# Pacing the modulation columns over a whole feed-forward half, the latent part of its last slab included

## The chip, the cores and the metric

One core of a Trainium2 chip runs the program. The metric is the device time of one execution in microseconds, as the median of several runs. One more execution was profiled; its time and its span, from the first instruction to the last, are given beside the runs.

## What is computed

Two layers of a diffusion backbone run over 256 context tokens and 256 latent tokens of width 1024, in float32. Each layer is a half-step SwiGLU feed-forward, a token mixer (gated DeltaNet, differential attention and SSD on one input, merged by gates), and a second half-step feed-forward. Each of the three is modulated by columns that come from a conditioning vector: nine groups of 1024 per layer and per kind of token.

```python
for i in range(DEPTH):                       # 2
    mx = (silu(c) @ w_ada[i] + b_ada[i]).reshape(bsz, 9, 1, 1024)     # latent tokens
    mc = (silu(c_ctx) @ w_ada[i] + b_ada[i]).reshape(9, 1024)         # context tokens
    x = x + half_ffn(x, ng[0], ng[1], mx[:, 0], mx[:, 1], mx[:, 2], w_ffn_in[i, 0], w_ffn_out[i, 0])
    ctx = ctx + half_ffn(ctx, ng[0], ng[1], mc[0], mc[1], mc[2], w_ffn_in[i, 0], w_ffn_out[i, 0])
    hx = modulate(rms_norm(x, ng[2]), mx[:, 3], mx[:, 4])             # h * (1 + scale) + shift
    hc = modulate(rms_norm(ctx, ng[2]), mc[3], mc[4])
    yx, yc = token_mixing(hx, hc, not last, ...)
    x = x + mx[:, 5] * rms_norm(yx, ng[3])
    x = x + half_ffn(x, ng[4], ng[5], mx[:, 6], mx[:, 7], mx[:, 8], w_ffn_in[i, 1], w_ffn_out[i, 1])
    ...                                      # the same for ctx, except in the last layer
# half_ffn(h, ...) = 0.5 * gate * rms_norm(swiglu(modulate(rms_norm(h, g_pre), shift, scale), w1, w2), g_post)
```

The result is x after both layers.

## The kernel before

Below, ffn(l, 0) and ffn(l, 1) are the two feed-forward halves of layer l, and mix(l) is the mixer between them. A segment is the 256 context tokens (segment 0) or the 256 latent ones (segment 1).

**Products.** Every weight block goes the same way (`wload`, from L133). A DMA on SyncE's queue brings it into a `raw` tile (three of them), ScalarE rounds it into a hi tile `whi` (L93), and VectorE writes the remainder into a lo tile `wlo` (L102); there are two of each. TensorE multiplies with both (L114): for each of eight contraction steps the hi weight by the hi and the lo activations, then the lo weight by the hi activations. In the mixer every third weight block uses a pair of `araw` tiles for hi and lo in the place of `whi` and `wlo`.

**A feed-forward half** (`ffn`). The 22 tiles of 128 hidden columns are cut into three slabs of 8, 7 and 7. For each hidden tile the inner function `hidden` makes two products from two weight blocks. ScalarE applies Silu to the first (`gS`), VectorE multiplies the two (`gV`, L96), ScalarE rounds `gV` into a `B` tile (L93), and VectorE writes the lo part of it into another (L102). When a slab's hidden tiles are done, eight output products follow that read all of the slab's `B` tiles. Slabs 0 and 1 take both segments together. Slab 2 takes them one after the other: first the context, whose end (`tail(0)`: norm of the output, addition to x, norm for the next stage) is then woven piece by piece into the latent part through `rest`, and then the latent tokens, whose end is woven into the next stage. The first `early` hidden tiles of slab 0 are made by segment too.

**Norms** (`rms`, from L370). TensorE sums the squares over the partitions, GpSimd raises to the power (L382), and VectorE writes a diagonal (L111) into a `gx` tile, which TensorE multiplies with ones to spread it over the partitions.

**Modulation columns** (`ada_block`, from L272). The list `todo` holds blocks in the order of their use, (layer, group, one of eight contraction steps). A block is one DMA of 512 KB into an `araw` tile, of which there are two, and then four scalar_tensor_tensor instructions on VectorE (L291): for each kind of token and each half of the block one product with the condition and a sum along the row, which goes into the columns `mod` or `part`. The elementwise product itself is not used. For the latent tokens it is written back over the `araw` tile, for the context tokens into a `gx` tile, of which there are two, the same two that the diagonals take in turn. Where only the latent tokens need the columns, a block has two instructions. After the eighth block of a group four small additions bring in `part` and the bias. `ada_block` also starts the next block's DMA.

**What sets the pace.** `due` is the number of blocks up to the half's goal: 48 in ffn(0,0), 40 in ffn(0,1), 40 in ffn(1,0), and none in ffn(1,1). Each `tick(share)` adds share times `due` to a credit and issues a block for each whole unit of it. A block is issued with a shifted priority, so that the scheduler may place it ahead of work that was written earlier, as far as its tiles are free. `whole` is the number of shares: two for a hidden tile of slabs 0 and 1 beyond the `early` ones, one for an output product of these slabs, and in slab 2 one for a hidden tile and a half for an output product, but in the context part only. `need(l, j)` issues at once whatever blocks up to (l, j) are still missing.

The vectors, masks and tables that mix(0) reads are loaded behind the DMA of the last modulation block (`vectors`, L227).

Of the kernel before, what the change touches and what calls it, by code (L numbers as in the profile page):

```python
# [58 lines left out]
class Net:  # L59
# [388 lines left out]
    def ffn(self, l, half, hl, segs, tail, mid):  # L448

        io = self.io
        y = [None] * KD
        one = [(s * SEG, (s + 1) * SEG) for s in segs]
        both = (one[0][0], one[-1][1])
        goal = ((0, 7), (1, 3), (1, 8), (1, 8))[2 * l + half]
        self.due, self.credit = sum(e[:2] <= goal for e in self.todo), 0
        self.left = self.due  # L460
        if self.due and (l, half) != (0, 0):
            self.ada_load(segs)
        early = 4 + 2 * l + half if len(segs) == 2 else 0
        whole = 2 * (15 - early) + 16 + (11 if len(segs) == 2 else 0)

        def hidden(k, k0, gu, a, b):
            pg, pu = self.proj([io["w_ffn_in"][l, half, k, i] for i in range(2)], hl, a, b)
            sg = self.t("gS", [P, T], 2)
            self.act(sg[:, a:b], pg[:, a:b], AF.Silu)
            f = self.t("gV", [P, T], 2)  # L470
            self.mul(f[:, a:b], sg[:, a:b], pu[:, a:b])
            hi, lo = self.rows(gu, k - k0, a, b)
            self.split(hi, lo, f[:, a:b])

        for si, (k0, k1) in enumerate(SLABS):
            nk = k1 - k0
            gu = self.newh()
            if si == 0:
                self.pace = 4
                for a, b in one:  # L480
                    for k in range(early):
                        with self.tc.issue_after(self.first.ins) if self.first else nullcontext():
                            hidden(k, k0, gu, a, b)
                        self.first = None
                    self.rest(None)
                    self.pace = 0
            src = io["w_ffn_out0"][l, half] if si == 0 else io["w_ffn_out1"][l, half, si - 1]
            for a, b in one if si == 2 else [both]:
                for k in range(k0 + (early if si == 0 else 0), k1):
                    hidden(k, k0, gu, a, b)  # L490
                    self.rest(2)
                    if si < 2:
                        self.tick(2 / whole)
                    elif a == 0:
                        self.tick(1 / whole)
                acc = {}
                for m in range(KD):
                    w = self.wload(src[m], nk * P)
                    o = self.ps("mm")
                    self.gemm(o[:, a:b], w, nk, P, gu, a, b, late=m == 0)  # L500
                    if si == 0:
                        y[m] = self.p()
                        self.act(y[m][:, a:b], o[:, a:b])
                    else:
                        self.add(y[m][:, a:b], y[m][:, a:b], o[:, a:b])
                    self.rest(1)
                    if si == 2:
                        self.squares(y, a // SEG, m, acc)
                        if a == 0:
                            self.tick(0.5 / whole)  # L510
                    else:
                        self.tick(1 / whole)
                if si == 2:
                    self.later(tail(a // SEG, y, acc))
            if si == 1:
                mid()


    def small_proj(self, l, hl):
# [987 lines left out]
```

## Time and profile before

| | us |
|---|---|
| three runs | 2545.96, 2547.03, 2553.83 |
| median | 2547.03 |
| the profiled execution | 2554.7 |
| its span | 2552.9 |
| TensorE busy in the span | 2431.2 |
| VectorE busy | 1820.8 |
| ScalarE busy | 1161.4 |
| GpSimd busy | 289.8 |

The profiled execution is one of its own, 7.7 us above the median of the others. Busy times leave out register, branch and DMA-issuing instructions. TensorE's weight loads run beside its products and are counted apart. In the rows further down PE is TensorE, DVE is VectorE, ACT is ScalarE and POOL is GpSimd; what stands in brackets at a row's end is the idle time of the engine before it and what ended that. Neighbouring rows overlap a little, since an engine starts an instruction before the one ahead of it has ended.

### The profile page before, as it was taken

The page shows a single profiled execution, that of the slowest core. Times are in us where ns is not written, and L with a number is a line of the kernel's source. Part 1 is how long each engine was busy: PE and PEld are TensorE (multiplying, and loading weights), DVE is VectorE, ACT ScalarE, POOL GpSimd, SP SyncE. Part 2 cuts the span into 40 slices and gives each one's busy share as a digit, 9 for nine tenths or more (in the row PEclk, how much of TensorE's full clock was granted, in tenths as well). Part 3 has the DMA queues.
Part 4 walks back from the last instruction along what each step waited for, and adds up shares of the span by engine and source line. Part 5 has one row for each costly group of instructions (what it writes and reads, how often), then busy time and mean ns, then how long its engine had stood idle before and what let it go on. Part 6 is the DMA issues. An engine that isn't in the chain of part 4 may idle for free. (4 is left out here: it accounts for less than half of the span.)

```text
span 2552.9 us, 40594 instructions
## 1 busy us (share of the span) xinstructions
PE 2431.2 (95%) x15546; PEld 2125.0 (83%) x15546; DVE 1820.8 (71%) x3826; ACT 1161.4 (45%) x1935; POOL 289.8 (11%) x288
## 2 busy tenths in 40 slices
PE   5999999999999999989999999999999889998998
PEld 3978799777788767888889998889988779887997
DVE  6888558899874564588964798634788977665455
ACT  4422256656443443563323563223566544454443
POOL 2000002202100011220000230000231120011001
PEclk8999999999999999999999999999999999998999
DMA  7766456443212312656754558734554342443664
GB/s 249 229 212 219 152 178 202 141 149 96 88 58 67 132 59 81 186 162 224 246 159 152 181 179 270 258 99 150 179 185 139 92 110 92 157 132 119 189 187 134
DMA packets 150498, 401.62 MB, mean 157 GB/s; under 512 B 39584, under 2 KB 50592, under 8 KB 150304
## 3 DMA queue, kind: packets, MB, share of 16 engines
q1 hardware_dynamic: 150304, 399.03, 49.8%
q8 instruction: 122, 2.00, 0.3%
q14 instruction: 72, 0.59, 0.1%
HBM read 383.76 MB, written 15.20 MB: 156 GB/s over the span
## 5 line engine op out<-in xcount | busy, mean ns | idle before, releaser
L114 PE MATMUL mm<-B,whi 128*128 128x256 f32 (+1 forms) x7632 | 1337.7, 325 | 28.8 <-ACT B L93 11.6
L114 PEld LDWEIGHTS mm<-B,whi 128*128 128x128 f32 x7632 | 1123.1, 190 | 155.7 <-ACT B L93 15.4
L93 ACT ACTIVATE whi<-raw 128x1024 fp32r<-128x1024 f32 (+1 forms) x506 | 524.5, 1037 | 611.9 <-PE mm L114 558.0
L102 DVE TENSOR_TENSOR wlo<-raw,whi 128x1024 fp32r<-128x1024 f32 (+1 forms) x506 | 613.4, 1213 | 177.1 <-ACT whi L93 147.1
L114 PE MATMUL mm<-B,wlo 128*128 128x256 f32 (+1 forms) x3816 | 696.6, 322 | 5.9 <-DVE wlo L102 5.9
L114 PEld LDWEIGHTS mm<-B,wlo 128*128 128x128 f32 x3816 | 567.3, 189 | 65.2 <-DVE wlo L102 7.7
L114 PE MATMUL mm<-B,araw 128*128 128x512 f32 (+1 forms) x1104 | 225.3, 352 | 4.2 <-DVE araw L102 4.2
L114 PEld LDWEIGHTS mm<-B,araw 128*128 128x128 f32 x1104 | 177.3, 191 | 31.4 <-DVE araw L102 5.6
L291 DVE SCALAR_TENSOR_TENSOR araw<-araw,P 128x512 f32<-128x512 f32 x264 | 173.0, 686 | 26.8 <-DMA araw<-in_w_ada 26.8
L291 DVE SCALAR_TENSOR_TENSOR gx<-araw,P 128x512 f32<-128x512 f32 x200 | 131.3, 687 | 44.5 <-DMA araw<-in_w_ada 44.0
L99 POOL TENSOR_TENSOR gm<-gm,ge 128x256 f32<-128x256 f32 x33 | 33.7, 1020 | 1127.0 <-ACT ge L93 1127.0
L93 ACT ACTIVATE B<-gV 128x256 fp32r<-128x256 f32 (+1 forms) x124 | 58.1, 469 | 226.2 <-DVE gV L96 226.1
L96 DVE TENSOR_TENSOR gV<-gS,mm 128x256 f32<-128x256 f32 (+1 forms) x124 | 59.7, 482 | 114.2 <-PE mm L114 99.7
L99 DVE TENSOR_TENSOR P<-P,mm 128x256 f32<-128x256 f32 (+1 forms) x88 | 43.2, 491 | 105.5 <-PE mm L114 105.5
L105 DVE SCALAR_TENSOR_TENSOR cv<-xp,vec,cv 128x512 f32<-128x512 f32 (+1 forms) x160 | 111.6, 706 | 2.1 <-ACT cv L93 1.4
L93 ACT ACTIVATE gS<-mm 128x256 f32<-128x256 f32 (+1 forms) x172 | 75.5, 439 | 35.8 <-PE mm L114 33.8
L102 DVE TENSOR_TENSOR araw<-raw,araw 128x1024 fp32r<-128x1024 f32 x56 | 70.0, 1251 | 25.8 <-PE mm L114 13.7
L93 ACT ACTIVATE araw<-raw 128x1024 fp32r<-128x1024 f32 x56 | 59.3, 1059 | 59.5 <-PE mm L114 43.2
L99 POOL TENSOR_TENSOR P<-P,gV 128x512 f32<-128x512 f32 (+1 forms) x30 | 36.1, 1202 | 241.6 <-DVE gV L105 238.1
L102 DVE TENSOR_TENSOR B<-gV,B 128x256 fp32r<-128x256 f32 (+1 forms) x124 | 62.3, 503 | 0.0
L93 ACT ACTIVATE B<-gR,mod 128x256 fp32r<-128x256 f32 x88 | 42.8, 501 | 33.5 <-DVE gR L105 33.1
L102 POOL TENSOR_TENSOR B<-gK,B 128x256 fp32r<-128x256 f32 x44 | 44.1, 1002 | 87.6 <-ACT gK L93 87.6
(265 smaller groups left out, 2180.7 us busy)
## 6 DMA issues: line engine op xcount, KB each, us to landing
raw<-in_w_ffn_in SPq DMA_DIRECT2D x248, 512.0 KB, 3.8
raw<-in_w_in SPq DMA_DIRECT2D x144, 512.0 KB, 3.6
araw<-in_w_ada SPq DMA_DIRECT2D x132, 512.0 KB, 4.4
raw<-in_w_ffn_out SPq DMA_DIRECT2D x88, 448.0 KB, 3.3
raw<-in_w_ffn_out SPq DMA_DIRECT2D x32, 512.0 KB, 4.3
raw<-in_w_branch SPq DMA_DIRECT2D x24, 512.0 KB, 3.5
raw<-in_w_out SPq DMA_DIRECT2D x24, 512.0 KB, 3.9
P<-keep SPq DMA_DIRECT2D x20, 256.0 KB, 5.5
```

The lines of the kernel that those rows point to most:

```text
L93: self.nc.scalar.activation(out=out, in_=in_, func=func, **kw)
L96: (eng or self.nc.vector).tensor_tensor(out, a, b, op=ALU.mult)
L99: (eng or self.nc.vector).tensor_tensor(out, a, b, op=ALU.add)
L102: (eng or self.nc.vector).tensor_tensor(out, a, b, op=ALU.subtract)
L105: self.nc.vector.scalar_tensor_tensor(out, a, s, b, op0=op0, op1=op1)
L114: self.nc.tensor.matmul(out, lhsT=lhsT, rhs=rhs, start=start, stop=stop)
L291: self.nc.vector.scalar_tensor_tensor(o, wh, 1.0, self.cond[s][h], op0=ALU.mult, op1=ALU.mult, accum_out=c)
```

## The change

`whole` now has 11 shares for each segment in the half, so both parts of slab 2 count: 60 shares instead of 49 in ffn(0,0), 58 instead of 47 in ffn(0,1), and 56 instead of 45 in ffn(1,0). The latent part of slab 2 ticks as the context part does. At the end of the half `need` issues what would be left up to the goal. No block is added or taken out.

```diff
--- before.py
+++ after.py
@@ -461,7 +461,7 @@
         if self.due and (l, half) != (0, 0):
             self.ada_load(segs)
         early = 4 + 2 * l + half if len(segs) == 2 else 0
-        whole = 2 * (15 - early) + 16 + (11 if len(segs) == 2 else 0)
+        whole = 2 * (15 - early) + 16 + 11 * len(segs)
 
         def hidden(k, k0, gu, a, b):
             pg, pu = self.proj([io["w_ffn_in"][l, half, k, i] for i in range(2)], hl, a, b)
@@ -491,7 +491,7 @@
                     self.rest(2)
                     if si < 2:
                         self.tick(2 / whole)
-                    elif a == 0:
+                    else:
                         self.tick(1 / whole)
                 acc = {}
                 for m in range(KD):
@@ -506,14 +506,14 @@
                     self.rest(1)
                     if si == 2:
                         self.squares(y, a // SEG, m, acc)
-                        if a == 0:
-                            self.tick(0.5 / whole)
+                        self.tick(0.5 / whole)
                     else:
                         self.tick(1 / whole)
                 if si == 2:
                     self.later(tail(a // SEG, y, acc))
             if si == 1:
                 mid()
+        self.need(*goal)
 
 
     def small_proj(self, l, hl):
```

Three places in the order of VectorE's instructions show what moves. Numbers behind a name are running numbers of tiles, and they differ between the two kernels.

The first is the end of slab 0 in ffn(0,0): the last lo weight (`wlo`) of the slab's last hidden tile, and the multiply that makes that tile (`gV`). Before:

```order
L102 TENSOR_TENSOR wlo_275_1325<-raw_273_1322,whi_274_1324 128x1024
L291 SCALAR_TENSOR_TENSOR gx_359_1744,mod0_0_75<-araw_353_1728,P_2_90 128x512
L99 TENSOR_TENSOR mod0_0_75<-mod0_0_75,part0_287_1402 128x8
L99 TENSOR_TENSOR mod0_1_76<-mod0_1_76,part1_288_1403 128x8
L291 SCALAR_TENSOR_TENSOR araw_353_1728,mod0_1_76<-araw_353_1728,P_4_92 128x512
L291 SCALAR_TENSOR_TENSOR gx_360_1746,part0_357_1742<-araw_353_1728,P_3_91 128x512
L99 TENSOR_TENSOR mod0_0_75<-mod0_0_75,bada_1_81 128x8
L99 TENSOR_TENSOR mod0_1_76<-mod0_1_76,bada_1_81 128x8
L291 SCALAR_TENSOR_TENSOR araw_353_1728,part1_358_1743<-araw_353_1728,P_5_93 128x512
L291 SCALAR_TENSOR_TENSOR gx_372_1820,mod0_0_75<-araw_356_1740,P_2_90 128x512
L291 SCALAR_TENSOR_TENSOR gx_373_1822,part0_357_1742<-araw_356_1740,P_3_91 128x512
L96 TENSOR_TENSOR gV_266_1302<-gS_265_1300,mm_264_1251 128x512
```

Now:

```order
L102 TENSOR_TENSOR wlo_272_1317<-raw_270_1314,whi_271_1316 128x1024
L291 SCALAR_TENSOR_TENSOR araw_360_1788,part1_298_1469<-araw_360_1788,P_5_93 128x512
L291 SCALAR_TENSOR_TENSOR araw_347_1712,part1_298_1469<-araw_347_1712,P_5_93 128x512
L99 TENSOR_TENSOR mod0_0_75<-mod0_0_75,part0_297_1468 128x8
L99 TENSOR_TENSOR mod0_1_76<-mod0_1_76,part1_298_1469 128x8
L99 TENSOR_TENSOR mod0_0_75<-mod0_0_75,bada_1_81 128x8
L99 TENSOR_TENSOR mod0_1_76<-mod0_1_76,bada_1_81 128x8
L96 TENSOR_TENSOR gV_263_1294<-gS_262_1292,mm_261_1243 128x512
```

Between the two, six modulation instructions (L291) became two.

The second is the latent part of slab 2 of ffn(0,0), from the diagonal of tail(0) on (L111, `gx<-cst`). Before:

```order
L111 TENSOR_SCALAR gx_693_3545<-cst_70,str_691_3541,stq_692_3542 128x128 x2
L102 TENSOR_TENSOR wlo_711_3634<-raw_709_3631,whi_710_3633 128x1024
L96 TENSOR_TENSOR gV_703_3615<-gS_702_3613,mm_701_3564 128x256
L102 TENSOR_TENSOR wlo_714_3640<-raw_712_3637,whi_713_3639 128x1024
L102 TENSOR_TENSOR B_522_2571<-gV_703_3615,B_521_2570 128x256
L105 SCALAR_TENSOR_TENSOR gR_705_3621<-P_277_1353,post0_517_2562,ps_704_3619 128x256
L105 SCALAR_TENSOR_TENSOR gR_707_3626<-P_285_1398,post0_517_2562,ps_704_3619 128x256
L105 SCALAR_TENSOR_TENSOR cv_719_3699<-P_295_1441,post0_517_2562,ps_704_3619 128x256
L99 TENSOR_TENSOR P_7_103<-P_7_103,gR_707_3626 128x256
L105 SCALAR_TENSOR_TENSOR cv_721_3705<-P_303_1482,post0_517_2562,ps_704_3619 128x256
L102 TENSOR_TENSOR wlo_725_3714<-raw_723_3711,whi_724_3713 128x1024
```

Now:

```order
L111 TENSOR_SCALAR gx_668_3477<-cst_70,str_666_3473,stq_667_3474 128x128 x2
L291 SCALAR_TENSOR_TENSOR gx_687_3567,mod0_0_75<-araw_651_3389,P_2_90 128x512
L102 TENSOR_TENSOR wlo_691_3576<-raw_689_3573,whi_690_3575 128x1024
L291 SCALAR_TENSOR_TENSOR gx_688_3569,part0_685_3565<-araw_651_3389,P_3_91 128x512
L291 SCALAR_TENSOR_TENSOR araw_651_3389,mod0_1_76<-araw_651_3389,P_4_92 128x512
L96 TENSOR_TENSOR gV_678_3547<-gS_677_3545,mm_676_3496 128x256
L105 SCALAR_TENSOR_TENSOR gR_680_3553<-P_274_1345,post0_494_2500,ps_679_3551 128x256
L105 SCALAR_TENSOR_TENSOR gR_682_3558<-P_282_1386,post0_494_2500,ps_679_3551 128x256
L102 TENSOR_TENSOR B_499_2509<-gV_678_3547,B_498_2508 128x256
L99 TENSOR_TENSOR P_7_103<-P_7_103,gR_682_3558 128x256
L102 TENSOR_TENSOR wlo_694_3582<-raw_692_3579,whi_693_3581 128x1024
```

After the diagonal 32 modulation instructions now stand in this part, the first at once; before there were none. Up to slab 1's end the running count of L291 is 224 before and 192 now, and between slab 1's end and the diagonal there is none in either order. In ffn(0,1) the same holds of 28 instructions. In ffn(1,0) none has moved to such a place.

The third is the end of that part, where the lo half of the mixer's first weight block is written (L102, `araw`). Before:

```order
L102 TENSOR_TENSOR wlo_815_4217<-raw_813_4214,whi_814_4216 128x896
L105 SCALAR_TENSOR_TENSOR B_116_432<-gR_817_4243,mod0_0_75,B_115_431 128x256
L99 TENSOR_TENSOR gm_779_4026<-gm_779_4026,cvo_805_4173 128x256
L102 TENSOR_TENSOR araw_828_4296<-raw_826_4293,araw_827_4295 128x1024
L99 TENSOR_TENSOR P_327_1605<-P_327_1605,mm_809_4182 128x256
L102 TENSOR_TENSOR wlo_831_4314<-raw_829_4311,whi_830_4313 128x1024
L99 TENSOR_TENSOR gm_779_4026<-gm_779_4026,gm_773_3991 128x256
L99 TENSOR_TENSOR P_335_1646<-P_335_1646,mm_816_4220 128x256
L96 TENSOR_TENSOR gm_821_4268<-gx_820_4266 128x128
L102 TENSOR_TENSOR wlo_839_4346<-raw_837_4343,whi_838_4345 128x1024
```

Now:

```order
L102 TENSOR_TENSOR wlo_831_4314<-raw_829_4311,whi_830_4313 128x1024
L111 TENSOR_SCALAR stv_833_4332<-ps_832_4329 128x2
L291 SCALAR_TENSOR_TENSOR gx_817_4241,mod0_0_75<-araw_801_4158,P_2_90 128x512
L105 SCALAR_TENSOR_TENSOR stq_835_4334<-str_834_4333,stv_833_4332 128x1 x2
L291 SCALAR_TENSOR_TENSOR gx_818_4243,part0_685_3565<-araw_801_4158,P_3_91 128x512
L111 TENSOR_SCALAR stq_835_4334<-stq_835_4334 128x2
L102 TENSOR_TENSOR wlo_839_4346<-raw_837_4343,whi_838_4345 128x1024
L291 SCALAR_TENSOR_TENSOR araw_801_4158,mod0_1_76<-araw_801_4158,P_4_92 128x512
L291 SCALAR_TENSOR_TENSOR araw_801_4158,part1_686_3566<-araw_801_4158,P_5_93 128x512
L99 TENSOR_TENSOR mod0_0_75<-mod0_0_75,part0_685_3565 128x8
L102 TENSOR_TENSOR araw_828_4296<-raw_826_4293,araw_827_4295 128x1024
```

The lo half now stands behind the last modulation instructions and behind two `wlo` that used to follow it.

## Rows read from the trace of the kernel before

**Rows 1.** The page, part 1: busy time, share of the span, instructions of each engine.
```profile
PE 2431.2 (95%) x15546; PEld 2125.0 (83%) x15546; DVE 1820.8 (71%) x3826; ACT 1161.4 (45%) x1935; POOL 289.8 (11%) x288
```

**Rows 2.** Waits of TensorE, 140 to 320 us: us in total, times, longest us.
```profile
PE mm L114 <- ACT B L93: 5.7, 2, 3.9
```

**Rows 3.** Table by stretches, line L291 alone: length, VectorE busy (count), granted clock, DMA.
```profile
260.00:280.00 20.00, 12.66 (x40) 1.00 0.70 218
280.00:300.00 20.00, 0.00 (x0) 0.91 0.32 103
1300.00:1320.00 20.00, 1.90 (x6) 1.00 0.53 154
```

**Rows 4.** Timeline of VectorE, end of slab 0 of ffn(0,0): start, duration, instruction [idle before].
```profile
149.12 0.69 DVE L291 SCALAR_TENSOR_TENSOR gx<-araw,P 128x512 f32<-128x512 f32 x1 [0.81 <-DMA araw<-in_w_ada]
...
152.50 0.68 DVE L291 SCALAR_TENSOR_TENSOR gx<-araw,P 128x512 f32<-128x512 f32 x1
...
153.11 0.68 DVE L96 TENSOR_TENSOR gV<-gS,mm 128x512 f32<-128x512 f32 x1
```

**Rows 5.** Timeline of TensorE, end of slab 0 of ffn(0,0).
```profile
148.78 1.79 PE L114 MATMUL mm<-B,wlo 128*128 128x512 f32 x7
...
156.60 4.89 PE L114 MATMUL mm<-B,whi 128*128 128x512 f32 x16
161.33 2.02 PE L114 MATMUL mm<-B,wlo 128*128 128x512 f32 x8
163.19 3.89 PE L114 MATMUL mm<-B,whi 128*128 128x512 f32 x16
```

**Rows 6.** Timeline of TensorE, end of slab 1 of ffn(0,0).
```profile
278.01 1.65 PE L114 MATMUL mm<-B,wlo 128*128 128x512 f32 x6 [0.22 <-DVE wlo L102]
...
283.42 4.20 PE L114 MATMUL mm<-B,whi 128*128 128x512 f32 x14
287.46 1.79 PE L114 MATMUL mm<-B,wlo 128*128 128x512 f32 x7
289.08 3.42 PE L114 MATMUL mm<-B,whi 128*128 128x512 f32 x14
```

**Rows 7.** Timeline of TensorE, end of slab 1 of ffn(0,1).
```profile
1327.03 0.64 PE L114 MATMUL mm<-B,whi 128*128 128x512 f32 x2
```

**Rows 8.** Table by stretches, all engines: length, busy time (count) of each, clock, DMA.
```profile
394.04:440.24 46.20, 46.20 (x388) 45.96 (x387) 40.28 (x71) 29.08 (x54) 15.30 (x14) 1.00 0.65 204
1436.75:1503.24 66.49, 65.36 (x543) 64.67 (x541) 56.73 (x105) 40.33 (x73) 23.83 (x23) 1.00 0.53 164
154.00:160.00 6.00, 4.93 (x14) 3.74 (x15) 5.97 (x15) 1.99 (x3) 0.00 (x0) 0.72 0.43 139
446.00:456.00 10.00, 8.60 (x40) 6.80 (x39) 8.80 (x23) 6.30 (x11) 3.74 (x5) 1.00 0.66 213
318.00:361.00 43.00, 43.00 (x359) 42.91 (x358) 23.37 (x30) 19.55 (x28) 0.00 (x0) 1.00 0.55 170
```

**Rows 9.** Timeline of VectorE, latent part of slab 2 of ffn(0,0).
```profile
393.44 0.60 DVE L111 TENSOR_SCALAR gx<-cst,str,stq 128x128 f32<-128x128 f32 x2
...
398.23 0.42 DVE L102 TENSOR_TENSOR B<-gV,B 128x256 fp32r<-128x256 f32 x1
...
405.27 0.96 DVE L102 TENSOR_TENSOR B<-gV,B 128x256 fp32r<-128x256 f32 x1
...
439.10 1.21 DVE L102 TENSOR_TENSOR araw<-raw,araw 128x1024 fp32r<-128x1024 f32 x1
```

**Rows 10.** Timeline of TensorE, first products of mix(0).
```profile
440.71 2.90 PE L114 MATMUL mm<-araw,B 128*128 128x512 f32 x12
...
451.04 0.70 PE L114 MATMUL ps<-gx,cst 128*128 128x256 f32 x2 [1.40 <-DVE gx L111]
```

**Rows 11.** Timeline of TensorE, start of ffn(1,0).
```profile
1499.09 3.25 PE L114 MATMUL mm<-B,whi 128*128 128x256 f32 x26
1503.30 0.62 PE L114 MATMUL mm<-B,wlo 128*128 128x256 f32 x3 [0.96 <-DVE wlo L102]
```

## The prediction

> **What bounds the kernel now.** I read the page's first part to see which engine fills the span, then TensorE's waits, then the timelines of TensorE and VectorE at the places where the modulation blocks stand thick, and last the table by stretches for VectorE's spare time. TensorE is busy for 95% of the span, VectorE for 71% [rows 1]. So time can be won only where TensorE waits, and lost only where something new makes it wait. From 140 to 320 us TensorE has just two waits of weight, both for a hidden tile that ScalarE splits [rows 2]: one at the end of slab 0 of the first feed-forward half, one at the end of slab 1. In front of each, VectorE works on modulation blocks. Four of its scalar_tensor_tensor instructions (L291) make a block, or two where only the latent tokens need it. They start 0.61 us apart, as from 152.50 to 153.11 [rows 4].
>
> Where those instructions stand decides everything. In the first half they fill 12.7 of 20 us up to 280 and stop dead there [rows 3]. In the second half they have nearly run out before slab 1 ends: 1.9 us between 1300 and 1320 [rows 3].
>
> Now the rule of the schedule, seen in the two orders of VectorE. The change gives 11 of its shares to the latent part of slab 2. A block issued there takes a `gx` tile for its context sum, and the ring of two `gx` tiles also serves the diagonal that tail(0)'s norm builds. So these blocks cannot be hoisted over that diagonal, while all the earlier ones are hoisted as before. The result is no even pace. After the change 160 of 192 instructions' worth of blocks still run ahead, nothing runs from slab 1's end to the diagonal, though VectorE is busy for only 23.4 of 43 us at 318 to 361 [rows 8], and the last 32 instructions (eight blocks) come bunched into the latent part. In ffn(0,1) it is 28 (seven blocks). In ffn(1,0) and ffn(1,1) the order has the same blocks at the same places: nothing for those.
>
> **The sum, part by part.** It is made against the profiled execution, 2554.7 us (span 2552.9 and 1.8 around it). The median of the runs shown is 2547.03, the profiled one lies 7.7 above it; I carry the difference over to the median.
>
> *A, slab 0's end of ffn(0,0).* From the start of the last lo matmuls of the old group to the full start of the next, TensorE takes 156.60 - 148.78 = 7.82 us; undisturbed it is 163.19 - 161.33 = 1.86 [rows 5]. That is 5.96 lost. The sixteen matmuls after it take 4.89 instead of 163.19's 3.89, 1.0 more, with the granted clock at 0.72 over 154 to 160 [rows 5, 8]. Between the hidden tile's last lo weight and its multiply (gV) stood six L291; now two, and since the start of the half six fewer have run: 6 x 0.614 = 3.7 us earlier. With the clock's 1.0 that is **-4.7**. Ends: 0, if VectorE only waits longer for a block's DMA, as it did for 0.81 us at 149.12 [rows 4]; -7.0, if the whole stall goes.
>
> *B, slab 1's end of ffn(0,0).* 283.42 - 278.01 = 5.41 against 289.08 - 287.46 = 1.62, so 3.8, and 4.20 against 3.42 for fourteen matmuls, 0.8 [rows 6]. No L291 is left there in the new order. The same place in ffn(0,1), where hardly any stand today, passes with no wait shown [rows 7]. So all of it goes: **-4.6**.
>
> *C, the latent part of ffn(0,0).* From the diagonal's end (393.44 + 0.60 = 394.04) to the end of the mixer's first lo block (439.10 + 1.21, less the overlap of neighbouring rows: 440.24) VectorE has 46.2 us [rows 9, 8]. It is busy for 40.3 of them; 5.9 are idle [rows 8]. New: 32 x 0.614 = 19.7, the four small adds of the block set 0.4, and two lo blocks and some small rows that used to stand behind the mixer's lo block and now stand ahead of it, 4.0. The lo block has to come after them, since its two `araw` tiles are the ones that the last two blocks free. With the idle time used up: 40.3 + 19.7 + 0.4 + 4.0 = 64.4, which puts the lo block at 458.4. TensorE needs it after the eight hi matmuls of the twelve that start at 440.71, about 442.6 [rows 10]. That is 15.8 late. The wait of 1.4 that TensorE has at 451.04 for the next diagonal [rows 10] goes into it: **+14.4**. Ends: +9, if TensorE's later waits and VectorE's lighter load behind it return 5; +23, if half of the idle can't be filled (2.9) and GpSimd collides more (5.8, below).
>
> *D, the latent part of ffn(0,1).* 66.5 us, VectorE busy for 56.7 [rows 8]. New: 28 x 0.614 = 17.2, adds 0.4, and one add that moves ahead, 0.4. 74.7 puts the second lo block of ffn(1,0) at 1436.75 + 74.7 = 1511.5; TensorE took it at 1503.30 after waiting 0.96 [rows 11]. That is 8.2, and ten hi matmuls of the next tile which TensorE had done ahead (1.2 of the 3.25 us of 26 [rows 11]) are now behind: **+9.4**. Ends: +4, +14, by the same reasons.
>
> *Edits that cost nothing.* The final `need` finds no block left: the shares add to the full count before it. The vector and mask loads that wait for the last modulation DMA move with it into the latent part; what reads them stands in the mixer, behind its first weights, so I price them at nothing; without that cover it is one load's landing, a few us. The SP queue gets no DMA more. Block loads come at one per 5.8 us in C (46.2 / 8), and the DMA queues are 0.65 busy there [rows 8]: no new bound. The second half's slab 0 keeps its order.
>
> Sum: -4.7 - 4.6 + 14.4 + 9.4 = **+14.5**, so 2554.7 becomes 2569.2, and the median 2547.0 becomes **2561.5**.
>
> **Two prices that could differ.** First the collisions of VectorE with GpSimd. One and the same lo split takes 0.42 us at 398.23 and 0.96 at 405.27, while GpSimd adds run around it [rows 9]. GpSimd has 14 instructions in the stretch of C [rows 8]; if the added instructions bring ten more collisions of 0.54, C is 5.4 larger, if all fourteen, 7.6. I take none: the 14 GpSimd instructions are there before as well and 40.3 already holds what they cost; the middle goes into the upper end as 5.8.
> The Trainium skill's page "SBUF — State Buffer" ("SBUF: two separate sides") says that a VectorE instruction with two SBUF inputs and a GpSimd instruction that reads SBUF hold a shared port pair exclusively, and the later one waits in full. By that rule each added instruction, which has two SBUF inputs, may hold up a GpSimd add or be held by it, and the sum would be about 2567 to 2569 instead of 2561.5. The two lengths above agree with it.
>
> Second the clock. After the wait of 3.9 us [rows 2] that ends at 154.5 the grant is 0.72 over 6 us, so part of them lies at 1.2 GHz and the rest at 2.4; after the 1.40 us at 451.04 it stays at 1.00 [rows 8, 10]. The new 24 us of waiting will come in many pieces, one ahead of each lo weight. I take them as short, no price. If two of them are as long as 3.9 us, each costs 1.0 as in A: +2.
> The skill's page "TensorE: Matmul & The Clock Gate" ("HAM oscillation") says that gaps in TensorE's work throw it back to half speed; by it the sum would be nearer 2565, if the waits come in long pieces.
>
> **Rivals.**
> 1. *The debt never reaches TensorE: faster.* Only A and B would count, 2547 - 9.3 = 2538. It takes that VectorE finds 20 us in the latent part. For it: VectorE is at 71% over the span. Against it: in just these 46 us it has 5.9 idle [rows 8], and TensorE waits for its lo weight at 1503.30 already [rows 11]. It is decided where the lo rows stand against the moment TensorE asks. Chance 0.09.
> 2. *Largely given back: within 0.3% (7.6 us, about what a measurement of this kernel can tell from no change).* If A goes whole (-7.0), C comes to +9 and D to +4: +1.4, 2548. For it: the mixer has waits of its own behind 451 [rows 10]. Against it: it needs three low ends at once. Chance 0.15.
> 3. *The change doesn't do what it says,* an even pace without any bunching, hidden by idle VectorE time: the orders speak against it; where it held, the result would be as in rival 1. It is counted there.
> 4. *More loss than the sum:* collisions and clock on top, +23 in C and +14 in D, A not moving: -4.6 + 37 = +32, 2579. Chance 0.06.
>
> **How the numbers follow.** The forecast, +14.5, has 0.70; with rival 4 that makes slower by over 0.3% 0.76, within 0.3% 0.15, faster 0.09. The forecast's own ends: with 2.3 more in A, 4 less in C, 3 less in D it is +5; with 5.8 in C, 2.9 of idle and 4 in D it is +27. The range from 2548 to 2575 leaves out rival 1 and some of 2 below, rival 4 above, about 2 in 10.
>
> **What would show it.** Right: no modulation instruction on VectorE between slab 1's end and the diagonal near 385, then 32 within 60 us with VectorE over 95% busy; TensorE waiting for lo weights or hidden tiles through that stretch, some 15 us in sum, the largest before the mixer's first lo matmuls; 8 to 9 us alike at the start of ffn(1,0); the stall at slab 1's end gone, the one at slab 0's end down to about 2 us. Wrong: TensorE without waits in the latent part although the 32 instructions stand there, which would mean that VectorE has more room than its busy time says; or modulation instructions spread over 281 to 390, which would mean that the ring doesn't hold them.

## The result, and the profile after

Over six runs each on one chip the changed kernel takes 2572.67 us (2570.18 to 2579.57), the kernel before 2552.51 us (2545.96 to 2555.90). The ratio is 1.0091, 95% interval 1.0078 to 1.0104, so the change costs 20 us by the medians and some 23 by the ratio. The profiled execution took 2576.2 us, 21.5 us more than that of before. The forecast was slower, by 14.5 us.

The page's first part of the changed kernel, against [rows 1]:

```profile
PE 2442.6 (95%) x15546; PEld 2132.4 (83%) x15546; DVE 1821.8 (71%) x3826; ACT 1166.7 (45%) x1935; POOL 287.1 (11%) x288
```

The busy times are the same within one per cent. Even so TensorE's matter: with the same 15546 matmuls it is busy for 11.4 us more, and idle for 10.1 us more (131.8 in a span of 2574.4 for 121.7 in 2552.9). So the added time is about half waiting and half matmuls that took longer; the longer ones that are shown below ran at a lower granted clock. To see where, I line the two executions up by ScalarE's rounding of the weight blocks, which has 562 instances in both, in the same sequence but for two neighbours at the mixer's start. Four of them, first in the kernel before, then in the changed one (timeline of ScalarE: start, duration, instruction, idle before it):

```profile
381.01 1.06 ACT L93 ACTIVATE whi<-raw 128x1024 fp32r<-128x1024 f32 x1 [1.09 <-PE mm L114]
...
528.09 1.06 ACT L93 ACTIVATE araw<-raw 128x1024 fp32r<-128x1024 f32 x1 [1.27 <-PE mm L114]
...
1444.65 1.06 ACT L93 ACTIVATE whi<-raw 128x1024 fp32r<-128x1024 f32 x1 [0.60 <-ACT ge L93]
...
1590.56 1.06 ACT L93 ACTIVATE whi<-raw 128x1024 fp32r<-128x1024 f32 x1 [2.37 <-PE mm L114]
```

```profile
370.39 1.06 ACT L93 ACTIVATE whi<-raw 128x1024 fp32r<-128x1024 f32 x1 [1.04 <-PE mm L114]
...
535.15 1.06 ACT L93 ACTIVATE araw<-raw 128x1024 fp32r<-128x1024 f32 x1 [1.29 <-PE mm L114]
...
1447.41 1.06 ACT L93 ACTIVATE whi<-raw 128x1024 fp32r<-128x1024 f32 x1
...
1608.13 1.06 ACT L93 ACTIVATE whi<-raw 128x1024 fp32r<-128x1024 f32 x1 [3.91 <-PE mm L114]
```

The first pair stands in the latent part of slab 2 of ffn(0,0): the change is 10.6 us ahead. The second stands in mix(0): 7.1 us behind. Between them it lost **17.7 us**. The third stands in the latent part of ffn(0,1), 2.8 behind, and the fourth behind slab 0 of ffn(1,0), 17.6 behind: **14.8 us** lost between them. So three amounts carry the result: -10.6, +17.7 and +14.8, together 21.9 of the 21.5. The last one has two places. Up to the first products of ffn(1,0) that take both segments, 12.2 are lost; the other 2.6 go at the end of its slab 0 (the rows are shown below). Smaller steps elsewhere (-4.4 from 1062 to 1210 us, +4.6 and -2.7 in mix(1), +1.8 in ffn(1,1)) nearly cancel. Of these the step of -4.4 shows in most of the other kernels as well, e1 included, whose second half is that of before, so it belongs to the profiled execution of before; the others come and go, and I leave them unexplained.

**The gain: the ends of slabs 0 and 1.** TensorE in the changed kernel, the same two places as [rows 5, 6]:

```profile
149.30 1.80 PE L114 MATMUL mm<-B,wlo 128*128 128x512 f32 x7
150.94 0.63 PE L114 MATMUL mm<-B,whi 128*128 128x512 f32 x2
151.41 0.39 PE L114 MATMUL mm<-B,wlo 128*128 128x512 f32 x1
151.63 3.90 PE L114 MATMUL mm<-B,whi 128*128 128x512 f32 x16
...
157.24 3.90 PE L114 MATMUL mm<-B,whi 128*128 128x512 f32 x16
...
272.04 1.56 PE L114 MATMUL mm<-B,wlo 128*128 128x512 f32 x6
273.44 0.63 PE L114 MATMUL mm<-B,whi 128*128 128x512 f32 x2
273.90 0.40 PE L114 MATMUL mm<-B,wlo 128*128 128x512 f32 x1
274.14 3.43 PE L114 MATMUL mm<-B,whi 128*128 128x512 f32 x14
...
279.04 3.43 PE L114 MATMUL mm<-B,whi 128*128 128x512 f32 x14
```

No row has a wait in brackets, and the sixteen matmuls from 151.63 take 3.90, the full clock's length; those of before took 4.89. From one slab end to the next the change goes from 0.5 us behind (149.30 for 148.78) to 5.95 ahead (157.24 for 163.19): 6.5 at the first place. At the second it comes to 10.0 ahead (279.04 for 289.08): 4.1 more.

**The loss at the mixer's start.** Where the modulation instructions stand now (table by stretches, L291 alone; the count holds the short accumulator reads too, two rows to an instruction):

```profile
284.00:383.00 99.00, 0.00 (x0) 1.00 0.52 160
383.00:449.00 66.00, 21.11 (x64) 0.92 0.70 218
```

None for 99 us, then 32 in 66 us, as the order had it. All engines in the same stretch, from the diagonal's end to the end of the mixer's first lo block, the like for ffn(0,1), and two pieces of ten microseconds, one in each (PE, PEld, DVE, ACT, POOL, granted clock, DMA):

```profile
383.24:448.86 65.62, 54.49 (x404) 51.19 (x402) 63.80 (x147) 32.85 (x58) 16.77 (x16) 0.92 0.70 218
1439.25:1516.91 77.66, 68.03 (x535) 65.50 (x534) 75.15 (x166) 40.93 (x73) 21.99 (x23) 0.96 0.58 182
436.00:446.00 10.00, 5.82 (x18) 4.89 (x19) 8.45 (x25) 4.67 (x8) 2.50 (x3) 0.50 0.65 213
1515.00:1525.00 10.00, 9.94 (x58) 9.68 (x59) 8.73 (x18) 6.23 (x11) 2.14 (x2) 0.69 0.60 184
```

VectorE is busy for 63.8 of 65.6 us, where it was for 40.3 of 46.2 [rows 8]. What TensorE does meanwhile:

```profile
436.57 1.86 PE L114 MATMUL mm<-B,wlo 128*128 128x256 f32 x7 [3.04 <-DVE wlo L102]
440.81 0.98 PE L114 MATMUL ps<-cst,gm 128*128 128x1 f32 x4 [2.38 <-DVE gm L99]
443.03 3.48 PE L114 MATMUL mm<-araw,B 128*128 128x512 f32 x8 [1.24 <-ACT araw L93]
448.99 1.74 PE L114 MATMUL mm<-araw,B 128*128 128x512 f32 x4 [2.49 <-DVE araw L102]
450.53 3.08 PE L114 MATMUL mm<-whi,B 128*128 128x512 f32 x8
453.45 1.08 PE L114 MATMUL mm<-wlo,B 128*128 128x512 f32 x4
454.37 2.02 PE L114 MATMUL mm<-whi,B 128*128 128x512 f32 x8
```

It waits 3.0 us for a lo weight, 2.4 for the squares' sum, 1.2 and 2.5 for the mixer's first hi and lo blocks. The granted clock over 436 to 446 is 0.50, which is the lower level of 1.2 GHz throughout, and the eight matmuls at 450.53, with everything there, take 3.08 where the next eight take 2.02.

**The loss at the start of ffn(1,0).** VectorE and then TensorE:

```profile
1478.43 1.22 DVE L291 SCALAR_TENSOR_TENSOR araw<-araw,P 128x512 f32<-128x512 f32 x1
...
1510.52 0.74 DVE L99 TENSOR_TENSOR gAV<-gAV,cvo 128x256 f32<-128x256 f32 x1 [1.41 <-ACT cvo L93]
...
1514.64 2.35 DVE L102 TENSOR_TENSOR wlo<-raw,whi 128x1024 fp32r<-128x1024 f32 x2
```

```profile
1514.86 0.99 PE L114 MATMUL ps<-cst,gAV 128*128 128x1 f32 x4 [6.47 <-DVE gAV L99]
1515.91 3.78 PE L114 MATMUL mm<-B,wlo 128*128 128x256 f32 x16
1519.48 1.05 PE L114 MATMUL ps<-gx,cst 128*128 128x256 f32 x2
1519.98 2.81 PE L114 MATMUL mm<-B,whi 128*128 128x256 f32 x16
1522.63 1.11 PE L114 MATMUL mm<-B,wlo 128*128 128x256 f32 x8
1523.57 2.06 PE L114 MATMUL mm<-B,whi 128*128 128x256 f32 x16
```

The two lo weights at 1514.64 end at 1516.9; TensorE has stood for 6.5 us before them. Afterwards sixteen lo matmuls take 3.78 and sixteen hi 2.81; at the full clock eight take 1.11 and sixteen 2.06. Over 1515 to 1525 the clock is 0.69.

**The end of slab 0 in ffn(1,0).** TensorE before, then in the changed kernel; the first row of each is the first product that takes both segments:

```profile
1557.04 3.90 PE L114 MATMUL mm<-B,whi 128*128 128x512 f32 x16
...
1585.00 0.49 PE L114 MATMUL mm<-B,whi 128*128 128x512 f32 x1 [0.49 <-ACT B L93]
...
1586.63 3.90 PE L114 MATMUL mm<-B,whi 128*128 128x512 f32 x16
```

```profile
1571.99 3.88 PE L114 MATMUL mm<-B,whi 128*128 128x512 f32 x16
...
1601.02 0.50 PE L114 MATMUL mm<-B,whi 128*128 128x512 f32 x1 [1.68 <-ACT B L93]
...
1602.67 5.43 PE L114 MATMUL mm<-B,whi 128*128 128x512 f32 x16
```

At the first row the changed kernel is 14.95 us behind, 12.2 more than in ffn(0,1). At the slab's end its wait is 1.2 longer and the sixteen matmuls behind it take 1.5 longer. That is a stall of the kind that slabs 0 and 1 of ffn(0,0) had before. e1 below loses 2.5 us at this place too, though it paces ffn(1,0) as the kernel before does, so these 2.6 us are not shown to come from the change.

### The profile page after: what moved, and what is told of

Read it like the earlier page. It is cut to its first block, busy times and chain, and to the rows that moved or that the text cites. A ratio compares the mean times of both kernels' runs of the same rounds, so it can differ in the third digit from the quotient of the medians.

```text
span 2574.4 us, 40582 instructions
## 1 busy us (share of the span) xinstructions
PE 2442.6 (95%) x15546; PEld 2132.4 (83%) x15546; DVE 1821.8 (71%) x3826; ACT 1166.7 (45%) x1935; POOL 287.1 (11%) x288
## 5 line engine op out<-in xcount | busy, mean ns | idle before, releaser
L102 DVE TENSOR_TENSOR wlo<-raw,whi 128x1024 fp32r<-128x1024 f32 (+1 forms) x506 | 613.9, 1214 | 189.8 <-ACT whi L93 158.5
L114 PEld LDWEIGHTS mm<-B,wlo 128*128 128x128 f32 x3816 | 570.4, 190 | 70.0 <-DVE wlo L102 11.4
L291 DVE SCALAR_TENSOR_TENSOR araw<-araw,P 128x512 f32<-128x512 f32 x264 | 173.2, 687 | 29.7 <-DMA araw<-in_w_ada 29.5
L291 DVE SCALAR_TENSOR_TENSOR gx<-araw,P 128x512 f32<-128x512 f32 x200 | 131.8, 685 | 32.6 <-DMA araw<-in_w_ada 32.1
L102 DVE TENSOR_TENSOR araw<-raw,araw 128x1024 fp32r<-128x1024 f32 x56 | 70.0, 1250 | 26.9 <-PE mm L114 13.7
L102 DVE TENSOR_TENSOR B<-gV,B 128x256 fp32r<-128x256 f32 (+1 forms) x124 | 61.4, 495 | 0.0
L102 POOL TENSOR_TENSOR B<-gK,B 128x256 fp32r<-128x256 f32 x44 | 44.3, 1007 | 94.0 <-ACT gK L93 94.0
```

What stands on the lines that cost most here:

```text
L102: (eng or self.nc.vector).tensor_tensor(out, a, b, op=ALU.subtract)
L114: self.nc.tensor.matmul(out, lhsT=lhsT, rhs=rhs, start=start, stop=stop)
L291: self.nc.vector.scalar_tensor_tensor(o, wh, 1.0, self.cond[s][h], op0=ALU.mult, op1=ALU.mult, accum_out=c)
```

## The experiments

Theory 1: VectorE has no room in a latent part of slab 2, so what is put there is paid by TensorE, and the two places and the gain at the slabs' ends are independent. Lines left out of an edit are marked with dots. The rivals are given with each run. All ratios are against the kernel before on the same chip.

| run | median us | ratio | 95% interval |
|---|---|---|---|
| e1 first half only | 2559.88 | 1.0031 | 1.0015 to 1.0048 |
| e2 thin latent | 2539.77 | 0.9955 | 0.9938 to 0.9971 |
| e12 half width latent | 2552.50 | 1.0005 | 0.9996 to 1.0015 |
| e3 own junk, after | 2557.48 | 1.0021 | 1.0009 to 1.0033 |
| e5 paced after | 2569.84 | 1.0071 | 1.0050 to 1.0092 |
| e9 after, first block not wide | 2569.61 | 1.0060 | 1.0037 to 1.0084 |
| e10 paced after, first block not wide | 2561.22 | 1.0031 | 1.0018 to 1.0045 |
| e4 paced before | 2541.28 | 0.9955 | 0.9939 to 0.9971 |
| e6 paced before, gx | 2541.27 | 0.9961 | 0.9947 to 0.9975 |
| e7 light pace, gx | 2536.87 | 0.9945 | 0.9926 to 0.9965 |
| e8 no share in slab 2 | 2539.49 | 0.9958 | 0.9942 to 0.9973 |
| e11 light pace, slab ends spared | 2539.98 | 0.9951 | 0.9933 to 0.9969 |

### e1: the change in ffn(0,0) alone

```diff
+        both_parts = (l, half) in ((0, 0),)
-        whole = 2 * (15 - early) + 16 + 11 * len(segs)
+        whole = 2 * (15 - early) + 16 + (11 * (1 + both_parts) if len(segs) == 2 else 0)
...
-                    else:
+                    elif a == 0 or both_parts:
                         self.tick(1 / whole)
...
-                        self.tick(0.5 / whole)
+                        if a == 0 or both_parts:
+                            self.tick(0.5 / whole)
```

> The new shares hold in ffn(0,0) alone; ffn(0,1) and ffn(1,0) are paced as before. Theory 1 (what counts is VectorE's time in each latent part, and the two places add up): against the kernel before, TensorE gains some 10.6 us by the end of slab 1 of ffn(0,0), loses about 17.7 from the diagonal to the mixer's first products, and nothing happens at the start of ffn(1,0): about +7 us, ratio 1.003. Rival 2 (the loss is spread over the program, by other placements or loads): about the +21 us of the whole change, ratio 1.008.

Measured: 1.0031. The places add up: the profiled execution is 9.2 us behind at the middle of mix(0), 6.7 at the end of ffn(0,1), and still 6.7 after the start of ffn(1,0), where the change has lost 12.2 more. At the end of slab 0 there it comes to 9.2.

### e2 and e12: the same instructions, shorter

```diff
...
+                n = 8 if self.thin else T
-                self.nc.vector.scalar_tensor_tensor(o, wh, 1.0, self.cond[s][h], op0=ALU.mult, op1=ALU.mult,
-                                                    accum_out=c)
+                self.nc.vector.scalar_tensor_tensor(o[:, :n], wh[:, :n], 1.0, self.cond[s][h][:, :n],
+                                                    op0=ALU.mult, op1=ALU.mult, accum_out=c)
...
             for a, b in one if si == 2 else [both]:
+                self.thin = l == 0 and si == 2 and a > 0
...
```

> As the change, but the modulation instructions that are issued in a latent part sum over 8 of their 512 columns, which leaves the rest of these columns' sums out; their loads, tiles and waits are kept. Theory 1 (VectorE's time): 60 x about 0.45 = 27 us less on VectorE, both losses go and the 10.6 us at the ends of the slabs stay: 7 to 11 us faster than before, ratio 0.996 to 0.997. Rival 3 (the araw tiles that the mixer's first weights wait for, the two gx tiles, or the loads' traffic): all of that is as in the change, so 15 to 23 us slower than before, ratio 1.006 to 1.009.

e12 has `T // 2` in the place of 8.

> As e2, but the modulation instructions of a latent part sum over half of their columns (256 of 512; the other half is left out), so each takes some 0.33 us of VectorE in the place of 0.61 (e2's 0.09). Theory 1 with the clock (VectorE's idle time takes up the first part of the load, long waits add the lower clock to the rest): the first place 17.7 - 32 x 0.28 - 3.2 = 5.5, the second 14.8 - 28 x 0.28 - 2.6 = 4.4, the ends of the slabs -10.6: ratio 0.999 to 1.001. Rival 7 (each us of load costs the same, no threshold and no clock): between e2's 0.9955 and the change's 1.0091 by the duration, 1.0017 or more.

Measured: 0.9955 and 1.0005. With the loads, the tiles and the issue left as in the change and VectorE's time taken out, the change is a gain of about its 10.6 us; that excludes the loads' traffic as the main cause. It doesn't quite exclude the rest of rival 3, since a shorter instruction also gives its tile back sooner; e9 asks after that. The first loss is 2.8 us in e2 and 6.5 in e12, by the same lining up. The second, up to 1578 us, is 0.6 and 5.9; slab 0's end of ffn(1,0) adds 2.3 in e12 and nothing in e2. In e12 the two are 12.4 us for instructions that start 0.34 us apart, in the change 29.9 for 0.61: the cost rises faster than the load, and rival 7's 1.0017 lies outside the interval, though not far. The second place came out 1.5 us above what I had expected of it. The clock falls less than in the change: 0.90 over the ten microseconds in which the change had 0.50.

```profile
436.00:446.00 10.00, 9.34 (x37) 7.03 (x37) 7.53 (x25) 6.03 (x7) 0.00 (x0) 0.90 0.71 244
```

### e3: the junk out of the gx ring

```diff
-                o = wh if s == conds[-1] else self.t("gx", [P, T], 2)
+                x = self.cond[s][h]
+                o = wh
+                if s != conds[-1]:
+                    o = self.xp[h][:, :, 2:258]
+                    wh, x = (v.rearrange("p (s t) -> p s t", s=2) for v in (wh, x))
...
```

> As the change, but the product that is not used goes into the padded convolution tiles, idle in a feed-forward half, in the place of the gx ring, so no block waits for a diagonal. In the order no modulation instruction stands in a latent part any more; five and seven stand ahead of the last multiply of slab 0 in ffn(0,0) and six and four at the end of slab 1 in ffn(0,1). Theory 1: the losses of 17.7 and 14.8 go, the stall at slab 1's end of ffn(0,0) goes (-4), that at slab 0's end stays, one like it comes at slab 1's end of ffn(0,1) (+2 to +4): 2 us faster to 2 slower than before. Rival 4 (the later shares cost by themselves, wherever the ring puts them): as the change, +21.

Measured: 1.0021, beyond the upper end that I had given, 2 us or 1.0008. Both latent losses are gone, as theory 1 has it: the execution is 12.6 us ahead at the start of mix(0). The miss is in ffn(0,1): between slab 1's end and the middle of slab 2's context part it falls back by 19 us. I had overlooked that ffn(1,0)'s blocks are freed too; the scheduler hoists them that far, four to an output product and four to a hidden tile, and TensorE waits for lo weights:

```profile
1358.69 1.43 PE L114 MATMUL mm<-B,wlo 128*128 128x256 f32 x8 [3.54 <-DVE wlo L102]
...
1364.39 1.21 PE L114 MATMUL mm<-B,wlo 128*128 128x256 f32 x8 [1.07 <-DVE wlo L102]
```

### e4 and e6: a pace that is kept

```diff
+        self.raw_dma = None
...
-        self.nc.sync.dma_start(raw[:, :n], src)
+        self.raw_dma = self.nc.sync.dma_start(raw[:, :n], src)
...
-        self.ada_dma = self.nc.sync.dma_start(w, self.io["w_ada"][l, j * KD + k])
+        with self.tc.issue_after(self.raw_dma.ins) if self.raw_dma else nullcontext():
+            self.ada_dma = self.nc.sync.dma_start(w, self.io["w_ada"][l, j * KD + k])
```

This on the kernel before is e6; with e3's edit too it is e4.

> As the kernel before (49, 47, 45 shares, nothing in a latent part), with the product in the convolution tiles as in the last one, and each block's load issued behind the latest weight load, so that a block cannot run far ahead of its share. The order shows four or five of its instructions to an output product, four ahead of each multiply at the slabs' ends, and three or four to a hidden tile in the context part of slab 2. Theory 1: the stalls at slab 0's and slab 1's end of ffn(0,0) shrink by half (-3 to -6), the context part of slab 2 has just room for a block to a tile (0 to +3): 2 to 6 us faster than before. Rival 2: no gain, since the blocks' places do not matter on average.

> e4 without its other edit: the product goes into the gx ring again, only each block's load is put behind the latest weight load. Nothing is issued in a latent part, so the ring should not matter. Theory 1: as e4, ratio 0.995 to 0.996. Rival: the ring of gx costs by itself, ratio nearer 1.

Measured: 0.9955 and 0.9961, more than I had expected of e4. TensorE has no wait at the end of slab 0 (timeline of e4):

```profile
147.06 1.80 PE L115 MATMUL mm<-B,wlo 128*128 128x512 f32 x7
148.70 0.63 PE L115 MATMUL mm<-B,whi 128*128 128x512 f32 x2
149.16 0.39 PE L115 MATMUL mm<-B,wlo 128*128 128x512 f32 x1
149.39 3.90 PE L115 MATMUL mm<-B,whi 128*128 128x512 f32 x16
```

The gain there is whole, not half: four and four instructions ahead of the last multiply, in the place of six and six, are few enough. Slab 2's context part of ffn(0,0), now with a block to a hidden tile, gives 3.6 us back in e4's profiled execution (12.4 ahead at 344 us, 8.8 at 390). The ring by itself costs nothing that these intervals show.

### e5, e9 and e10: the even pace to the end, and the araw tiles

e5 is the change with both edits of e4.

> The change with both edits of e4: the unused product in the convolution tiles, and each block's load behind the latest weight load, so that the pace of 60, 58, 56 shares is really kept. No block waits for the gx ring, none is bunched behind a diagonal; the order leaves some 24 modulation instructions in the latent part of ffn(0,0) and some 20 in that of ffn(0,1), the rest spread. Theory 1 (VectorE has no room in a latent part, wherever the blocks wait): against e4 8 instructions fewer than the change had, so some 11 us lost at the first place and 5 at the second, less 3 for the lighter context part: 0 to 5 us slower than before, ratio 1.000 to 1.002. Rival 5 (only the bunching by the ring costs, an even pace to the end is free): as e4 or better, ratio 0.995.

Measured: 1.0071. Rival 5 falls: an even pace into the latent part is no cure. But I was wrong on the size too. At the first place it lost 19 us by 528 us, and 22 by 794, with fewer instructions than the change had, and VectorE was less full: busy for 61.2 of 65 us from 380 to 445. Another wait had come in, for the `araw` tile that the last blocks, now loaded late, gave free late (TensorE, timeline of e5):

```profile
451.75 2.07 PE L115 MATMUL mm<-araw,B 128*128 128x512 f32 x4 [5.63 <-DVE araw L103]
```

Whether the change has that wait as well is what e9 asks; e10 asks the same of e5.

```diff
+        self.spare = True
...
         more = self.wide and self.lo_turn % 3 == 0
+        if more and self.spare:
+            more, self.spare = False, False
```

> As the change, but the first weight block of mix(0) uses whi and wlo like its neighbours; the first that needs the araw tiles stands three blocks later. Theory 1 (VectorE's time alone): the 32 modulation instructions stand ahead of the mixer as before, the loss at the mixer's start stays: 17 to 23 us slower than before, ratio 1.007 to 1.009. Rival 3 (the wait for the araw tiles is the larger part of it): TensorE's waits of 1.2 and 2.5 us there and the clock that falls behind them go: 10 to 14 us slower than before, ratio 1.004 to 1.0055.

> e5 with the same edit. e5 lost 20 us at the mixer's start with 24 instructions there, where VectorE's busy time alone gave 11, and TensorE waited 1.6 and 5.6 us for the araw tiles' hi and lo halves. Rival 3, that the araw tiles, freed late by the last blocks, make up the difference: 9 us less than e5, ratio 1.003 to 1.004. Theory 1 (VectorE's time alone): as e5, 1.007.

Measured: 1.0060 and 1.0031. In e5 the tiles were the difference: without them the first place costs 9.2 us by 528 us, and 11.3 by 794, near the 11 from VectorE's time. For the change e9 decides less sharply. Its ratio lies between the two forecasts. By the lining up it has lost 14.9 us by 528 us and 19.3 by 794, the change 17.7 at either, and TensorE waits 4.1 us for the next `araw` block instead (waits of TensorE in e9, 400 to 470 us):

```profile
PE mm L115 <- DVE araw L103: 4.1, 1, 4.1
```

So these tiles are not the main part of the change's loss there; whether they hold up to some 3 us of it stays open.

### e7, e8 and e11: where the shares go

e7 is e6 with half a share for a hidden tile of slab 2's context part and none for its products; e8 is e4 with none in slab 2; e11 is e7 with no share at the last hidden tile of slabs 0 and 1.

```diff
-        whole = 2 * (15 - early) + 16 + (11 if len(segs) == 2 else 0)
+        whole = 2 * (15 - early) + 16 + (3.5 if len(segs) == 2 else 0)
...
-                        self.tick(1 / whole)
+                        self.tick(0.5 / whole)
...
-                            self.tick(0.5 / whole)
+                            self.tick(0 / whole)
```

> As e6, with half a share for a hidden tile of slab 2's context part and none for its output products (41.5, 39.5, 37.5 shares), so 16 of ffn(0,0)'s 192 instructions stand there in the place of 43, and the slabs before carry five to an output product. Theory 1: the 4.6 us that e4 lost in ffn(0,0)'s context part and the 2.5 in ffn(0,1)'s come back in most part, the ends of the slabs stay free of waits: 4 to 6 us faster than e4, ratio 0.993 to 0.994. Rival 6 (the slabs' ends fill again, seven instructions ahead of the last multiply of slab 0): A's wait comes back in part, no faster than e4.

> As e4, with no share at all in slab 2 (38, 36, 34 shares): all blocks stand in slabs 0 and 1, VectorE is nearly full there. Theory 1: slab 2's loss of 4.6 and 2.5 is gone, the output products with five or six instructions each make TensorE wait for lo weights now and then (0 to 6): ratio 0.993 to 0.997. Rival: the slabs' ends stall as before, ratio 1.

> As e7 (loads behind the latest weight load, half a share for a hidden tile of the context part of slab 2, none for its products), and no share at the last hidden tile of slabs 0 and 1, so that four and four instructions, not five and seven, stand ahead of the last multiply of slab 0 as in e4. Theory 1: e4's gain of 8 us at slab 0's end in the place of e7's 2, and e7's free context part: 16 to 20 us faster than before, ratio 0.992 to 0.994. Rival 6 (eight instructions ahead of the last multiply of slab 1 now make the wait there): as e7, 0.9945.

Measured: 0.9945, 0.9958, 0.9951. The three, e4 and e6 can't be told from each other by these intervals. Each trades one place for another. e7 keeps all it has in slab 2 and gets 2 us at slab 0's end where e4 got 8. e11 gets 7 there and pays at slab 1's end, where TensorE waits again (waits of TensorE in e11, 130 to 320 us), so rival 6 was right there:

```profile
PE mm L115 <- ACT B L94: 2.6, 1, 2.6
```

All five beat both kernels of the study, by some 0.4 to 0.55% against the one before.

## Why the prediction was right in its direction and wrong in its size

**A and B, the gains: right, a little small.** -9.3 was forecast, -10.6 came. A's whole stall went (6.5 with the clock's 1.0), where I had reckoned only the 3.7 us of six instructions off it and named 7.0 as the end. B gave 4.1 of its 4.6.

**C, the mixer's start: mechanism right, 14.4 forecast, 17.7 measured.** VectorE's stretch was worked out at 64.4 us and took 65.6, since 1.8 us of it could not be filled: +1.2. The step that failed is "I take them as short, no price", said of the waits and the clock. The waits came as 3.0, 2.4, 1.2 and 2.5 within 16 us, with none above 0.9 before them, and the clock went to 0.50. Of what that cost, the part behind the last wait counts: the four matmuls at 448.99 and the eight at 450.53 take 1.54 and 2.92 from start to start, where the same numbers took 0.91 and 1.86 at the full clock: +1.7. 14.4 + 1.2 + 1.7 = 17.3; the last 0.4 I can't place.

**D, the start of ffn(1,0): mechanism right, 9.4 forecast, 12.2 measured.** VectorE took 77.7 us from the diagonal to the second lo weight, not 74.7: 2.5 us stayed idle, 1.4 of them for ScalarE's square at 1510.52. My sum had used up all the idle time, though TensorE's and ScalarE's results were late there too: +3.0. Behind the wait of 6.5 us the clock stood at 0.69 over ten microseconds, and sixteen lo and sixteen hi matmuls took 3.57 and 2.65 from start to start, where 1.88 and 1.90 are the full clock's: +2.4. That makes 14.8, of which TensorE's rows have 13.7 (the lo product that starts at 1508.95 before starts at 1525.47 now, less the 2.8 that it was behind); why the other 1.1 don't show I can't say. Of the 13.7, 1.5 come back by 1571.99, since the kernel before has waits on that way which the changed one lacks, the longest of 0.7 us for a lo weight at 1544.28.

**ffn(1,0) itself: nothing forecast, 2.6 measured.** That "the order has the same blocks at the same places" holds at the end of slab 0: four modulation instructions stand ahead of its last multiply in both. In the changed kernel's profiled execution they start 0.5 us later, behind their loads, and three small instructions that close a block set have come in between; the clock fell behind the longer wait. As e1 loses 2.5 us there with this half paced as before, it is not shown that the change has to pay for it.

So the steps that failed are two terms of the sum, C and D: they filled all of VectorE's idle time, of which 1.8 and 2.5 us stayed idle, and they put the clock at nothing, which cost 1.7 and 2.4. With 3.3 more in C, 2.8 in D, 2.6 in ffn(1,0) and 1.3 more of gain, 14.5 becomes 21.9. I had both prices in the text, the clock's as +2 and the idle time's in the upper ends, and left both out of the sum. Two of its side figures are off as well, without touching the forecast: the middle of 5.4 and 7.6 is 6.5, not 5.8, and two waits at 1.0 each make 2563.5, where the text has 2565. The other price left out, collisions with GpSimd, was rightly left out: of the 60 modulation instructions in the two stretches only three ran beside a GpSimd instruction at all, and one was lengthened, 1.22 us at 1478.43.

The rule of the Trainium skill's page "TensorE: Matmul & The Clock Gate" ("HAM oscillation"), that gaps throw TensorE back to half speed, leaned the right way; the trace agrees with it at 0.50 and 0.69. By the rule of the Trainium skill's page "SBUF — State Buffer" ("SBUF: two separate sides") a VectorE instruction with two SBUF inputs and a GpSimd instruction that reads SBUF shut each other out. With three meetings in 60 the trace doesn't bear out the price that I drew from it, and doesn't speak against the rule either.

The carrying over was a part of the miss as well. I carried the sum from the profiled execution of before onto a median of three runs, 2547.03; the median of six is 2552.51. Of the 14.5 us forecast that leaves 9.0 between 2561.5 and what the kernel before takes.

**The rivals.** That the debt never reaches TensorE, and that it is given back: neither. After 478 us nothing of the first loss comes back before 1050. Of the larger loss with collisions and clock on top, the clock came and the collisions did not. That the change doesn't do what it says was seen before the run, in the order, and holds: the blocks run as early as their loads allow, but for those behind the diagonal. e4 to e6 show that a pace has to be tied to something that the scheduler must wait for.

## What to carry to other kernels

Before work is spread over a further part of a program, read that part's idle time on the engine that does it, not the mean over the span: VectorE's 71% was 87% here and 54% one part earlier, because the context tokens' norms are woven into it. And look at what the order does with the work once it is issued: here a priority didn't hold the pace, a ring of two tiles did by accident, and tying the loads to the latest weight load held it on purpose. When VectorE goes from having idle time to being always late, leave some of its idle time unfilled in the sum, and price the lower clock that follows TensorE's waits.

## What was not expected of the hardware

A row of short waits brought TensorE's granted clock down as far as one long wait did. Over 436 to 446 us, with waits of 3.0, 2.4 and 1.2 us, it was 0.50; behind the single wait of 3.9 us in the kernel before it was 0.72 over six us, and one of 1.4 us had left it at 1.00 [rows 8, 10]. But the single wait of 6.5 us ahead of ffn(1,0) gave 0.50 as well (table by stretches of the changed kernel; the clock is the third number from the end):

```profile
1511.00:1521.00 10.00, 6.08 (x26) 5.85 (x27) 8.73 (x20) 4.06 (x7) 2.27 (x3) 0.50 0.33 105
```
